# Probability-value products on all 128 columns of TensorE: shared values as fp32r halves for both heads, fox values side by side in F32

## The chip, the cores and the metric

The kernel runs on one core of a Trainium2 chip. Its time is the device time of one execution in microseconds (us), three runs before the change: 3118.08 us median (3116.48 to 3119.01). The profiled execution took 3118.62 us. Engines: PE is TensorE (matmul, with PEld for its weight loads), DVE VectorE, ACT ScalarE, POOL GpSimd, SP the engine that issues the DMAs.

## The reference

The reference is a whole model for 512 tokens of width 1024: a first block (state-space branch, spatial gating, cross attention, feed-forward) and a second block of two layers with four branches each. The change touches three of those four branches, which are attentions with 8 heads of 64 columns. All compute softmax(q k^T + bias) v:

```python
def forgetting_attention(q, k, v, f_logit, f_bias):     # v: one set of 64 columns per head
    ...
    p = jax.nn.softmax(jnp.where(causal[None, None], logits, neg), axis=-1)
    return jnp.einsum('bhqs,bshd->bqhd', p.astype(v.dtype), v)
def dsa_attention(q, k, v, qi, ki, wi):                  # v: one set for all 8 heads, causal, top 128 keys
    ...
    return jnp.einsum('bhqk,bqkd->bqhd', p.astype(vg.dtype), vg)
def sliding_window_gqa(q, k, v, sinks):                  # v: one set for 4 heads, window of 128 keys
    ...
    out = jnp.einsum('bngrqk,bnkgd->bnqgrd', (p / denom).astype(vband.dtype), vband)
```

"Shared values" are those of the second (called DSA here) and the third (sliding window): both heads of a pair multiply their own probabilities with the same 64 columns. The first ("fox") has values of its own for each head.

## The kernel before

Almost all large products are done with split operands. An F32 matrix is cut into a high part that fits TensorE's fp32r format and a low part with the rest (`split`, line 164: a copy on ACT writes the high part, a subtraction on DVE or POOL the low one), and `mm3` (lines 187 to 191) issues three fp32r products (high x high, high x low, low x high) in place of one in F32. `gemm_b` and `gemm_a` run this over the contraction; weights come by DMA as "raw" and are split on the fly.

Each of the two layers of the second block is `mix2` (line 1302). It projects the 512 tokens into queries, keys and values, and runs the four branches. Softmax work is written as Python generators (`attend`, line 952), one per pair of heads; `pump` takes a few steps of the waiting generators between two projections, and `drain` runs one to its end. The build then orders the instructions of each engine with a timeline model of its own, so that the program order mixes the steps of several generators with the projections. Each engine takes its instructions strictly in that order.

`attend` treats the 512 queries in four chunks c of 128. For a chunk it computes the scores of both heads into a PSUM bank "sc" each (`score`: lines 1081 and 1082 for fox, 1093 and 1094 for the others), masks and takes the maximum on DVE (line 968), exponentials and their sum on ACT (through line 124), normalises on DVE (line 982), transposes the probabilities in blocks of 128x128 on PE (line 995), copies them out of PSUM on ACT (line 998, tile probT), and multiplies by the values (line 1003). A causal chunk c has c+1 key blocks, a window chunk two (the first one). In line 1003 the stationary operand is a value block of one head (128 keys x 64 columns), the moving operand 128 transposed probabilities, both F32; head 0 writes partitions 0 to 63 and head 1 partitions 64 to 127 of one bank "pv", which is held for the four chunks of a pair and evicted once, with one `split` of 128x512 (lines 1008 and 1009).

The values: fox values come from `natural` into four tiles h; the shared ones lie in msc, which holds 204 columns per chunk (64 for DSA, two sets of 64 for the window, then 4 and 8 columns for other uses).

The buffers that matter: PSUM banks "mm" (4, results of projections), "sc" (3, scores and transposes) and "pv" (1); SBUF tiles of 128x512 "g" (52, long-lived), "tmp" (10) and probT (3). A projection for the rotary branches leaves its "mm" bank by four copies on ACT (`rope`, line 925) and one product on DVE (line 927).

Of the kernel before, what the change touches and what calls it, by code (L numbers as in the profile page):

```python
# [9 lines left out]
F32 = mybir.dt.float32  # L10
F32R = mybir.dt.float32r
AF = mybir.ActivationFunctionType
ALU = mybir.AluOpType
# [17 lines left out]
NSLOT = 52  # L31
# [40 lines left out]
class Builder:  # L72
# [879 lines left out]
    def attend(self, ys, pair, score, mask, init, value, blocks, sinks=None):  # L952

        nc = self.nc
        pv = None
        pend = None
        for c in list(range(CHUNKS)) + [None]:
# [28 lines left out]
            if pend is not None:  # L986
                pc, bl, pt = pend
                if pv is None:
                    pv = self.bank("pv")
                n = len(bl)  # L990
                tt = []
                for i in range(2):
                    tr = self.bank("sc")
                    for j in range(n):
                        nc.tensor.transpose(tr[:, j * P:(j + 1) * P], pt[i][:, j * P:(j + 1) * P],  # L995
                                            self.ident)
                    ptT = self.t(self.ap, [P, S], "probT", bufs=3)
                    nc.scalar.copy(ptT[:, :n * P], tr[:, :n * P])  # L998
                    tt.append(ptT)
                yield  # L1000
                for j, b in enumerate(bl):
                    for i in range(2):
                        nc.tensor.matmul(pv[i * 64:(i + 1) * 64, pc * P:(pc + 1) * P],  # L1003
                                         value(i, b), tt[i][:, j * P:(j + 1) * P],
                                         start=j == 0, stop=j == n - 1)
                yield
            pend = nxt
        yh, yl = self.g(F32R), self.g(F32R)
        self.split(yh, yl, pv)
        ys[pair] = (yh, yl)  # L1010
        yield

    def fox_bias(self, l, msc):
# [5 lines left out]
        self.add(f, msc[:, :, 196:204], self.vec(f"fb{l}")[:, None, :].to_broadcast(n4))  # L1019
# [35 lines left out]
    def fox_pair(self, ys, pair, pq, pk, va):  # L1055
# [23 lines left out]
        def score(i, c, ps, k0, nk):  # L1079
# [5 lines left out]
                           lambda i, b: va[b][:, pair * P + i * 64:pair * P + i * 64 + 64],  # L1085
                           lambda c: list(range(c + 1)))

    def rope_pair(self, ys, pair, q, hh, ll, mask, init, value, blocks, sinks=None):
# [7 lines left out]
        return self.attend(ys, pair, score, mask, init, value, blocks, sinks)  # L1096

    def select(self, si, hh, ll, msc):
# [3 lines left out]
        nc.vector.tensor_scalar(wi, msc[:, :, 192:196], 0.0625, None, ALU.mult)  # L1102
# [199 lines left out]
    def mix2(self, l):  # L1302
# [19 lines left out]
        msc = self.t(ap, [P, CHUNKS, 204], "msc")  # L1322
# [276 lines left out]
```

## Time and profile before

| what | value |
|---|---|
| time, median of three runs | 3118.08 us |
| profiled execution, its own time | 3118.62 us |
| its span, first to last instruction | 3116.7 us |
| PE busy | 3031.5 us (97%) |
| DVE busy | 1884.2 us (60%) |
| ACT busy | 1352.9 us (43%) |
| POOL busy | 974.6 us (31%) |
| DMA | 287.10 MB, 29.6% of 16 engines' span |

A matmul's record in the trace is longer than the distance to the next one, because matmuls are pipelined: what one costs PE is read from the starts of its neighbours. An F32 matmul leaves two records, one in fp32r leaves one. "Idle before" is the time in which an engine stood still ahead of a group, with what ended it.

### The profile page before, as it was taken

Reading aid. Unit: us, or ns where it says so; the run is one execution under the profiler, and the core shown is the slowest. Engines: PE = TensorE matmul, PEld = TensorE weight load, DVE = VectorE, ACT = ScalarE, POOL = GpSimd, SP = SyncE. Lnnn points to the kernel's source line nnn. Section 1 sums busy time; section 2 is a strip of 40 time slices with the busy share of each in tenths; the row PEclk is TensorE's granted clock in tenths of the full one; section 3 lists DMA queues with packets and bytes.
Section 4 is the critical chain, followed back from the end, with each engine's and each line's share of the span. In section 5 each row is a group of like instructions: output and inputs, shape, how many; then the busy total and the mean of one; then the engine's idle time right before and its main releaser. Section 6 shows DMA issues by size and latency. Waiting matters only on the chain.

```text
span 3116.7 us, 39233 instructions
## 1 busy us (share of the span) xinstructions
PE 3031.5 (97%) x14922; PEld 2481.6 (80%) x14922; DVE 1884.2 (60%) x3423; ACT 1352.9 (43%) x2278; POOL 974.6 (31%) x594
## 2 busy tenths in 40 slices
PE   8998999999999999999999999999999999999998
PEld 6877878888887777778888888888677778888887
DVE  7899454454455596455456665548845455465575
ACT  5523343332224475646334333356555452343343
POOL 3234243210014442345454000054333445610011
PEclk9999999999999999999999999999999999999999
DMA  5223343223333321222223323242211222333332
GB/s 161 75 80 95 102 146 105 95 88 102 101 90 94 102 75 55 68 78 82 78 88 122 95 91 105 81 133 78 68 55 61 92 75 78 122 96 100 95 96 80
DMA packets 98075, 287.10 MB, mean 92 GB/s; under 512 B 11984, under 2 KB 20432, under 8 KB 97888
## 3 DMA queue, kind: packets, MB, share of 16 engines
q1 hardware_dynamic: 97888, 284.61, 29.6%
q8 instruction: 117, 1.92, 0.3%
q14 instruction: 70, 0.57, 0.1%
HBM read 274.64 MB, written 9.93 MB: 91 GB/s over the span
## 4 chain that ended last, share of the span: by engine, by line
PE 82%; DVE 11%; ACT 2%; DMA 2%; issue 2%; POOL 1%; SPq 0%; DVEq 0%; ACTq 0%; POOLq 0%
PE psmm L189 24%; PE psmm L190 24%; PE psmm L191 24%; DVE tmp L112 3%; PE pspv L1003 2%; DVE g L112 2%; PE pssc L995 1%; DVE g L1128 1%; DVE m L1127 1%; PE pssc L1093 1%; DVE tmp L1217 1%; PE pssc L1094 1%; DVE s5t L112 0%; PE pspv L791 0%; PE pssc L759 0%
## 5 line engine op out<-in xcount | busy, mean ns | idle before, releaser
L191 PE MATMUL psmm<-g,lo 128*128 128x512 f32 (+1 forms) x3456 | 1346.8, 390 | 4.0 <-POOL lo L112 4.0
L190 PE MATMUL psmm<-g,hi 128*128 128x512 f32 (+1 forms) x3456 | 1348.2, 390 | 1.5 <-DVE g L171 1.5
L189 PE MATMUL psmm<-g,hi 128*128 128x512 f32 (+1 forms) x3456 | 1346.4, 392 | 2.3 <-ACT g L167 1.3
L167 ACT CAST hi<-raw 128x1024 fp32r<-128x1024 f32 (+3 forms) x506 | 507.6, 1005 | 1035.3 <-PE psmm L190 748.5
L112 POOL TENSOR_TENSOR lo<-raw,hi 128x1024 fp32r<-128x1024 f32 (+1 forms) x259 | 630.6, 2436 | 1008.8 <-ACT hi L167 849.2
L191 PEld LDWEIGHTS psmm<-g,lo 128*128 128x128 f32 x3456 | 650.3, 188 | 138.4 <-POOL lo L112 5.3
L189 PEld LDWEIGHTS psmm<-g,hi 128*128 128x128 f32 x3456 | 650.2, 188 | 135.4 <-ACT hi L167 3.1
L190 PEld LDWEIGHTS psmm<-g,hi 128*128 128x128 f32 x3456 | 650.8, 188 | 132.3 <-issue 2.6
L112 POOL TENSOR_TENSOR tmp<-tmp,tmp 128x512 f32<-128x512 f32 (+1 forms) x121 | 166.8, 1381 | 1019.1 <-DVE tmp L1419 570.7
L112 DVE TENSOR_TENSOR lo<-raw,hi 128x1024 fp32r<-128x1024 f32 (+2 forms) x247 | 298.0, 1207 | 90.7 <-ACT hi L167 90.6
L112 DVE TENSOR_TENSOR tmp<-psmm,g 128x512 f32<-128x512 f32 x236 | 161.4, 688 | 295.9 <-PE psmm L191 248.3
L189 PE MATMUL psmm<-hi,g 128*128 128x512 f32 (+1 forms) x384 | 144.5, 384 | 16.4 <-ACT g L124 11.1
L1445 DVE SCALAR_TENSOR_TENSOR g<-psmm,g 128x512 f32<-128x512 f32 x88 | 60.7, 690 | 151.7 <-PE psmm L191 151.7
L124 ACT ACTIVATE prob<-prob,nmx 128x128 f32<-128x128 f32 (+2 forms) x192 | 102.5, 535 | 106.7 <-DVE nmx L968 105.9
L190 PE MATMUL psmm<-lo,g 128*128 128x512 f32 (+1 forms) x384 | 146.5, 384 | 2.4 <-POOL lo L112 2.4
L191 PE MATMUL psmm<-hi,g 128*128 128x512 f32 (+1 forms) x384 | 145.2, 382 | 0.0
L112 DVE TENSOR_TENSOR g<-tmp,g 64x512 fp32r<-64x512 f32 (+1 forms) x162 | 130.5, 806 | 14.1 <-ACT g L167 11.0
L124 ACT ACTIVATE tmp<-tmp 128x512 f32<-128x512 f32 (+1 forms) x138 | 84.2, 613 | 111.4 <-DVE tmp L112 98.5
L1419 DVE SCALAR_TENSOR_TENSOR tmp<-tmp,vec,tmp 128x511 f32<-128x511 f32 (+1 forms) x176 | 131.0, 746 | 2.0 <-ACT tmp L124 0.6
L998 ACT COPY probT<-pssc 128x128 f32<-128x128 f32 (+2 forms) x192 | 69.8, 397 | 88.3 <-PE pssc L995 83.3
L189 PEld LDWEIGHTS psmm<-hi,g 128*128 128x128 f32 x384 | 75.1, 196 | 29.2 <-ACT g L124 11.1
L982 DVE TENSOR_SCALAR prob<-prob,sm 128x128 f32<-128x128 f32 (+2 forms) x192 | 93.2, 527 | 2.5
(276 smaller groups left out, 3117.6 us busy)
## 6 DMA issues: line engine op xcount, KB each, us to landing
raw<-w_up SPq DMA_DIRECT2D x110, 512.0 KB, 3.5
raw<-w_gates SPq DMA_DIRECT2D x64, 512.0 KB, 3.5
raw<-w_down SPq DMA_DIRECT2D x72, 384.0 KB, 3.1
raw<-w_rope SPq DMA_DIRECT2D x40, 512.0 KB, 3.6
raw<-w_branch SPq DMA_DIRECT2D x32, 512.0 KB, 3.5
raw<-w_out SPq DMA_DIRECT2D x24, 512.0 KB, 3.6
raw<-w_gate SPq DMA_DIRECT2D x22, 512.0 KB, 3.7
raw<-w_fox SPq DMA_DIRECT2D x16, 512.0 KB, 3.5
```

Of the source, the lines that this page charges most:

```text
L112: (eng or self.nc.vector).tensor_tensor(out, a, b, op)
L124: self.nc.scalar.activation(out, in_, func, **k)
L167: nc.scalar.copy(hi, src)
L189: mm(out, sh, mh, start=start, stop=False)
L190: mm(out, sh, ml, start=False, stop=False)
L191: mm(out, sl, mh, start=False, stop=stop)
L982: nc.vector.tensor_scalar(pt[i][:, :nk], pt[i][:, :nk], sm[:, i:i + 1], None, ALU.mult)
L995: nc.tensor.transpose(tr[:, j * P:(j + 1) * P], pt[i][:, j * P:(j + 1) * P], self.ident)
L998: nc.scalar.copy(ptT[:, :n * P], tr[:, :n * P])
L1003: nc.tensor.matmul(pv[i * 64:(i + 1) * 64, pc * P:(pc + 1) * P], value(i, b), tt[i][:, j * P:(j + 1) * P], start=j == 0, stop=j == n - 1)
L1419: nc.vector.scalar_tensor_tensor(o[:, sh:], u[:, :S - sh], w, o[:, sh:], ALU.mult, ALU.add)
L1445: self.nc.vector.scalar_tensor_tensor(self.x[d], ps, 0.5, self.x[d], ALU.mult, ALU.add)
```

## The change

Shared values are split once, when they are projected, into high and low parts that lie side by side: 128 stationary columns in fp32r (tile vhl). The probabilities of both heads are transposed into one bank, next to each other (256 moving columns per key block), and split as well: a high part probT by a copy on ACT, a low part by a subtraction on DVE. One product with the high and one with the low probabilities then give, for both heads at once, high values in partitions 0 to 63 and low values in 64 to 127 of the "pv" bank; the two halves are added on the way out. Fox values stay F32, but the two heads' value columns stand side by side as 128 stationary columns, each head's 128 probabilities are multiplied with both, and of the result the half that belongs to the head is taken. As outputs take twice the room, the "pv" bank holds two chunks and is evicted twice per pair. There are five probT tiles, and four "g" tiles fewer.

```diff
-NSLOT = 52
+NSLOT = 48
+NPT = 5
...
-    def attend(self, ys, pair, score, mask, init, value, blocks, sinks=None):
+    def attend(self, ys, pair, score, mask, init, value, blocks, shared, sinks=None):
...
+        dt = F32R if shared else F32
...
             if pend is not None:
                 pc, bl, pt = pend
-                if pv is None:
+                n = len(bl)
+
+                tt = []
+                for j0 in range(0, n, 2):
+                    tr = self.bank("sc")
+                    w = min(2, n - j0) * 2 * P
+                    for k in range(w // P):
+                        j, i = j0 + k // 2, k % 2
+                        nc.tensor.transpose(tr[:, k * P:(k + 1) * P], pt[i][:, j * P:(j + 1) * P],
+                                            self.ident)
+                    th = self.t(self.ap, [P, S], "probT", dt, bufs=NPT)
+                    tl = self.t(self.ap, [P, S], "probT", dt, bufs=NPT) if shared else None
+                    nc.scalar.copy(th[:, :w], tr[:, :w])
+                    if shared:
+                        self.sub(tl[:, :w], tr[:, :w], th[:, :w].bitcast(F32))
+                    tt.append((th, tl))
+                yield
+                u = pc % 2
+                if u == 0:
                     pv = self.bank("pv")
-                n = len(bl)
-                tt = []
-                for i in range(2):
-                    tr = self.bank("sc")
-                    for j in range(n):
-                        nc.tensor.transpose(tr[:, j * P:(j + 1) * P], pt[i][:, j * P:(j + 1) * P],
-                                            self.ident)
-                    ptT = self.t(self.ap, [P, S], "probT", bufs=3)
-                    nc.scalar.copy(ptT[:, :n * P], tr[:, :n * P])
-                    tt.append(ptT)
+                if shared:
+                    out = pv[:, u * 256:(u + 1) * 256]
+                    for j, b in enumerate(bl):
+                        for z in range(2):
+                            nc.tensor.matmul(out, value(b), tt[j // 2][z][:, j % 2 * 256:j % 2 * 256 + 256],
+                                             start=j == z == 0, stop=j == n - 1 and z == 1)
+                else:
+                    for i in range(2):
+                        out = pv[:, u * 256 + i * P:u * 256 + i * P + P]
+                        for j, b in enumerate(bl):
+                            a = j % 2 * 256 + i * P
+                            nc.tensor.matmul(out, value(b), tt[j // 2][0][:, a:a + P],
+                                             start=j == 0, stop=j == n - 1)
                 yield
-                for j, b in enumerate(bl):
-                    for i in range(2):
-                        nc.tensor.matmul(pv[i * 64:(i + 1) * 64, pc * P:(pc + 1) * P],
-                                         value(i, b), tt[i][:, j * P:(j + 1) * P],
-                                         start=j == 0, stop=j == n - 1)
-                yield
+                if u:
+                    if yh is None:
+                        yh, yl = self.g(F32R), self.g(F32R)
+                    cs = slice(pc * P - P, pc * P + P)
+                    v = "p (u i n) -> p u i n"
+                    p4 = pv.rearrange(v, u=2, i=2)
+                    two = lambda x: x.rearrange("p (u n) -> p u n", u=2)
+                    if shared:
+                        t, y = self.tmp()[0:64], self.tmp()[:, :256]
+                        nc.scalar.copy(t, pv[64:128])
+                        t4 = t.rearrange(v, u=2, i=2)
+                        for i in range(2):
+                            self.add(two(y[i * 64:i * 64 + 64]), p4[0:64, :, i], t4[:, :, i])
+                        self.split(yh[:, cs], yl[:, cs], y)
+                    else:
+                        for i in range(2):
+                            r = slice(i * 64, i * 64 + 64)
+                            self.split(two(yh[r, cs]), two(yl[r, cs]), p4[r, :, i])
+                    yield
             pend = nxt
-        yh, yl = self.g(F32R), self.g(F32R)
-        self.split(yh, yl, pv)
         ys[pair] = (yh, yl)
-        yield
...
-                           lambda i, b: va[b][:, pair * P + i * 64:pair * P + i * 64 + 64],
-                           lambda c: list(range(c + 1)))
+                           lambda b: va[b][:, pair * P:(pair + 1) * P],
+                           lambda c: list(range(c + 1)), False)
...
-        msc = self.t(ap, [P, CHUNKS, 204], "msc")
-        self.natural(I["w_misc"][l], x, [msc[:, c] for c in range(CHUNKS)], 204, 2)
+        msc = self.t(ap, [P, CHUNKS, 12], "msc")
+        vhl = self.t(ap, [P, CHUNKS, 3, 2, 64], "vhl", F32R)
+        banks = self.gemm_a(I["w_misc"][l], x, 204, 2)
+        self.pump(self.rate)
+        for c in range(CHUNKS):
+            self.split(vhl[:, c, :, 0], vhl[:, c, :, 1], banks[c][:, :192].rearrange("p (v d) -> p v d", v=3),
+                       scale=self.rc[:, c:c + 1])
+            self.act(msc[:, c], banks[c][:, 192:204], AF.Copy, scale=self.rc[:, c:c + 1])
+        vals = lambda b, n: vhl[:, b, n].rearrange("p z d -> p (z d)")
```

The new order of the program on PE is shown at three places of the first layer. Lines 190 to 192 of the changed kernel are the old 189 to 191, 1003 is now the transposes' line (old 995), 1131 and 1132 are the old scores 1093 and 1094; 1019 and 1026 are the new products.

First, on PE, the first product of the first DSA pair; before:

```order
L190 MATMUL psmm_9829<-g_9753,hi_9825 128x512
L191 MATMUL psmm_9829<-g_9752,lo_9826 128x512
L1003 MATMUL pspv_9843<-probT_9846,msc_7999 64x128
L1003 MATMUL pspv_9843<-probT_9850,msc_7999 64x128
L190 MATMUL psmm_9935<-g_9753,hi_9825 128x512
```

and with the change:

```order
L191 MATMUL psmm_9842<-g_9702,hi_9838 128x512
L192 MATMUL psmm_9842<-g_9701,lo_9839 128x512
L1019 MATMUL pspv_9863<-probT_9859,vhl_8000 128x256
L1019 MATMUL pspv_9863<-probT_9860,vhl_8000 128x256
L191 MATMUL psmm_9950<-g_9702,hi_9838 128x512
```

One product per head with 64 columns became one per part of the probabilities, with 128 columns and both heads in the 256 moving columns.

Second, on PE, the second chunk of the second fox pair, where the head's products stood apart and a score product lay between; before:

```order
L1003 MATMUL pspv_8945<-probT_9055,h_8124 64x128
L1081 MATMUL pssc_9070<-g_8617,g_8615 128x512
L1082 MATMUL pssc_9070<-g_8621,g_8619 128x512
L191 MATMUL psmm_9871<-g_7705,lo_9875 128x512
L1003 MATMUL pspv_8945<-probT_9060,h_8124 64x128
L1003 MATMUL pspv_8945<-probT_9055,h_8125 64x128
L1003 MATMUL pspv_8945<-probT_9060,h_8125 64x128
```

and with the change:

```order
L192 MATMUL psmm_9769<-g_7711,hi_9772 128x512
L1026 MATMUL pspv_8960<-probT_9064,h_8133 128x128
L1026 MATMUL pspv_8960<-probT_9064,h_8134 128x128
L1026 MATMUL pspv_8960<-probT_9064,h_8133 128x128
L1026 MATMUL pspv_8960<-probT_9064,h_8134 128x128
L190 MATMUL psmm_9769<-g_7721,hi_9772 128x512
```

The number of products is the same, each writes 128 partitions, and they now follow each other.

Third, on PE, the third DSA pair between its second and its last chunk of scores (g_9315 and g_9316 before, g_9309 and g_9310 after, are its queries); before:

```order
L1093 MATMUL pssc_10337<-g_7895,g_9316 128x384
L1094 MATMUL pssc_10337<-g_7897,g_9316 128x384
L995 MATMUL pssc_10346<-idn_71,prob_10281 128x128
L1003 MATMUL pspv_10298<-probT_10301,msc_7999 64x128
L1003 MATMUL pspv_10298<-probT_10305,msc_7999 64x128
L995 MATMUL pssc_10346<-idn_71,prob_10281 128x128
L995 MATMUL pssc_10351<-idn_71,prob_10282 128x128 x2
L190 MATMUL psmm_10813<-g_7706,hi_10816 128x512
L191 MATMUL psmm_10813<-g_7705,lo_10817 128x512
L189 MATMUL psmm_10813<-g_7711,hi_10816 128x512
```

and with the change:

```order
L1131 MATMUL pssc_10383<-g_7895,g_9309 128x384
L1132 MATMUL pssc_10383<-g_7897,g_9309 128x384
L1131 MATMUL pssc_10387<-g_7895,g_9310 128x384
L1132 MATMUL pssc_10387<-g_7897,g_9310 128x384
L1003 MATMUL pssc_10369<-idn_71,prob_10316 128x128
L1019 MATMUL pspv_10376<-probT_10372,vhl_8000 128x256
L1003 MATMUL pssc_10410<-idn_71,prob_10332 128x128
L1131 MATMUL pssc_10436<-g_7895,g_9309 128x512
L1132 MATMUL pssc_10436<-g_7897,g_9309 128x512
L1003 MATMUL pssc_10410<-idn_71,prob_10333 128x128
L1003 MATMUL pssc_10410<-idn_71,prob_10332 128x128
L1003 MATMUL pssc_10410<-idn_71,prob_10333 128x128
```

Where 24 projection products followed the transposes, the next chunk's scores and transposes now follow at once, and from the second head's first score of the pair to its last chunk's transposes no projection product stands on PE.

## Rows read from the trace of the kernel before

**Rows 1.** The page: busy tenths of PE in 40 slices of the span, its granted clock in tenths of full speed, and the chain that ended last by engine and by line.

```profile
PE   8998999999999999999999999999999999999998
...
PEclk9999999999999999999999999999999999999999
...
PE 82%; DVE 11%; ACT 2%; DMA 2%; issue 2%; POOL 1%; SPq 0%; DVEq 0%; ACTq 0%; POOLq 0%
PE psmm L189 24%; PE psmm L190 24%; PE psmm L191 24%; DVE tmp L112 3%; PE pspv L1003 2%; DVE g L112 2%; PE pssc L995 1%; DVE g L1128 1%; DVE m L1127 1%; PE pssc L1093 1%; DVE tmp L1217 1%; PE pssc L1094 1%; DVE s5t L112 0%; PE pspv L791 0%; PE pssc L759 0%
```

**Rows 2.** Busy time in stretches with fox (1100 and 2155) and with shared values (1222): length, then busy us and instructions of PE, PEld, DVE, ACT and POOL, granted clock, DMA share, GB/s; then PE's waits in 1100 to 1225 and 2150 to 2280: us in total, times, longest.

```profile
1100.00:1222.00 122.00, 116.58 (x629) 89.58 (x627) 103.26 (x279) 78.26 (x167) 42.49 (x22) 1.00 0.21 65
1222.00:1585.00 363.00, 362.81 (x1941) 289.88 (x1941) 188.05 (x463) 174.95 (x368) 164.65 (x94) 1.00 0.24 76
2155.00:2277.00 122.00, 112.99 (x611) 86.24 (x610) 102.30 (x270) 75.65 (x161) 41.01 (x20) 1.00 0.20 63
...
PE pssc L995 <- DVE prob L982: 1.2, 1, 1.2
...
PE pssc L995 <- DVE prob L982: 4.8, 4, 2.2
```

**Rows 3.** Groups of PE's instructions by line and form: out<-in, rows*columns of the weights, moving operand, count, busy us, mean ns, idle before.

```profile
L1003 PE MATMUL pspv<-probT,msc 128*64 128x128 f32 x544 | 55.8, 287 | 0.0
L1003 PE MATMUL pspv<-probT,h 128*64 128x128 f32 x320 | 33.3, 286 | 4.6 <-ACT probT L998 4.1
```

**Rows 4.** PE's timeline around two stretches of old products, of four and of sixteen records: start in us, length, what.

```profile
1227.13 0.40 PE L191 MATMUL psmm<-g,lo 128*128 128x512 f32 x1
1227.46 0.44 PE L1003 MATMUL pspv<-probT,msc 128*64 128x128 f32 x4
1227.83 0.50 PE L190 MATMUL psmm<-g,hi 128*128 128x512 f32 x1
1228.16 0.39 PE L191 MATMUL psmm<-g,lo 128*128 128x512 f32 x1
1228.39 0.40 PE L190 MATMUL psmm<-g,hi 128*128 128x512 f32 x1
...
1248.32 0.39 PE L191 MATMUL psmm<-g,lo 128*128 128x512 f32 x1
1248.64 1.09 PE L1003 MATMUL pspv<-probT,msc 128*64 128x128 f32 x16
1249.66 0.33 PE L1093 MATMUL pssc<-g,g 128*128 128x128 f32 x1
1249.83 0.28 PE L1094 MATMUL pssc<-g,g 128*128 128x128 f32 x1
1249.94 0.33 PE L1093 MATMUL pssc<-g,g 128*128 128x256 f32 x1
```

**Rows 5.** PE's timeline where full-width products of the new forms stand already: fp32r with 256 moving columns (344), and F32 with 128 moving columns (line 1167, in the retention branch).

```profile
344.42 0.28 PE L189 MATMUL psmm<-g,hi 128*128 128x256 f32 x1
344.53 0.28 PE L190 MATMUL psmm<-g,hi 128*128 128x256 f32 x1
344.65 0.28 PE L191 MATMUL psmm<-g,lo 128*128 128x256 f32 x1
...
1536.76 0.39 PE L190 MATMUL psmm<-g,hi 128*128 128x512 f32 x1
1536.98 0.38 PE L1167 MATMUL pspv<-tmp,tmp 128*128 128x128 f32 x2
1537.20 0.56 PE L1171 MATMUL pspv<-h,tmp 128*128 128x64 f32 x4
1537.60 0.44 PE L1167 MATMUL pspv<-tmp,tmp 128*128 128x128 f32 x2
1537.87 0.56 PE L1171 MATMUL pspv<-h,tmp 128*128 128x64 f32 x4
```

**Rows 6.** Groups of DVE and ACT by line and form: out<-in, count, busy us, mean ns, idle before. Lines 968 and 982 are masking with maxima and normalising, "g<-pspv" the old eviction, 998 the copy of transposed probabilities, 925 a rotary copy.

```profile
L968 DVE CUSTOM_DVE_ANT_0 prob<-pssc,cst 128x128 f32<-128x128 f32 x32 | 9.1, 288 | 46.7 <-PE pssc L1094 36.4 <-PE pssc L1082 10.3
L968 DVE CUSTOM_DVE_ANT_0 prob<-pssc,g 128x256 f32<-128x256 f32 x16 | 6.5, 422 | 7.0 <-PE pssc L1094 7.0
L968 DVE CUSTOM_DVE_ANT_0 prob<-pssc,g 128x384 f32<-128x384 f32 x16 | 8.7, 554 | 2.5 <-PE pssc L1094 2.3
L968 DVE CUSTOM_DVE_ANT_0 prob<-pssc,g 128x512 f32<-128x512 f32 x16 | 10.7, 686 | 6.9 <-PE pssc L1094 6.9
L982 DVE TENSOR_SCALAR prob<-prob,sm 128x128 f32<-128x128 f32 x48 | 14.2, 333 | 0.6
L982 DVE TENSOR_SCALAR prob<-prob,sm 128x256 f32<-128x256 f32 x80 | 43.2, 582 | 1.0
L982 DVE TENSOR_SCALAR prob<-prob,sm 128x384 f32<-128x384 f32 x32 | 19.4, 646 | 0.3
L982 DVE TENSOR_SCALAR prob<-prob,sm 128x512 f32<-128x512 f32 x32 | 16.6, 559 | 0.5
L112 DVE TENSOR_TENSOR g<-pspv,g 128x512 fp32r<-128x512 f32 x32 | 22.0, 686 | 47.5 <-ACT g L167 47.5
L998 ACT COPY probT<-pssc 128x512 f32<-128x512 f32 x32 | 17.7, 586 | 25.4 <-PE pssc L995 21.9 <-PE pspv L1003 3.5
L925 ACT COPY tmp<-psmm 32x512 f32<-32x512 f32 x160 | 92.4, 578 | 2.4
```

More of the change, by code (lines that the diff above doesn't have):

```diff
@@ L949, in stack_k @@
         return hh, ll
-    def attend(self, ys, pair, score, mask, init, value, blocks, sinks=None):
+    def attend(self, ys, pair, score, mask, init, value, blocks, shared, sinks=None):
         nc = self.nc
+        dt = F32R if shared else F32
         pv = None
         pend = None
+        yh = yl = None
         for c in list(range(CHUNKS)) + [None]:
@@ L1006, in attend @@
-                yield
+                    th = self.t(self.ap, [P, S], "probT", dt, bufs=NPT)
[4 more added lines that the diff above has]
+                    tt.append((th, tl))
+                yield
+                u = pc % 2
+                if u == 0:
+                    pv = self.bank("pv")
@@ L1018, in fox_bias @@
         a = self.t(ap, n4, "fa")
-        self.add(f, msc[:, :, 196:204], self.vec(f"fb{l}")[:, None, :].to_broadcast(n4))
+        self.add(f, msc[:, :, 4:12], self.vec(f"fb{l}")[:, None, :].to_broadcast(n4))
         self.nc.vector.scalar_tensor_tensor(a, f, -1.0, f, ALU.mult, ALU.min)
@@ L1094, in score @@
             nc.tensor.matmul(ps, q[i][:, qs], ll[:, k0:k0 + nk], start=False, stop=True)
-        return self.attend(ys, pair, score, mask, init, value, blocks, sinks)
+        return self.attend(ys, pair, score, mask, init, value, blocks, True, sinks)
     def select(self, si, hh, ll, msc):
@@ L1101, in select @@
         wi = self.t(ap, [P, CHUNKS, 4], "wi")
-        nc.vector.tensor_scalar(wi, msc[:, :, 192:196], 0.0625, None, ALU.mult)
+        nc.vector.tensor_scalar(wi, msc[:, :, 0:4], 0.0625, None, ALU.mult)
         self.masks = {}
@@ L1347, in mix2 @@
                                      lambda c: self.maskc(c) if c == 0 else self.masks[c],
-                                     lambda i: 3e38, lambda i, b: msc[:, b, 0:64],
+                                     lambda i: 3e38, lambda b: vals(b, 0),
                                      lambda c: list(range(c + 1))))
@@ L1364, in mix2 @@
                 lambda i, j=j: nsk[:, 2 * j + i:2 * j + i + 1],
-                lambda i, b, hg=hg: msc[:, b, 64 + hg * 64:128 + hg * 64],
+                lambda b, hg=hg: vals(b, 1 + hg),
                 lambda c: [c] if c == 0 else [c - 1, c],
```

1 line of the change is left out of this document (removed).

## The prediction

> **What bounds the kernel now.** I read the page first [rows 1]: the slices show TensorE (PE) at 9 tenths or more almost everywhere and its granted clock at full speed, and the chain that ended last is 82% PE, three quarters of it the split-precision products of lines 189 to 191. What PE is given less to do is therefore worth its time, in a stage where PE does not wait. Next I cut out the stretches of the two attention layers in which probability times value (line 1003) runs [rows 2]. From 1222 to 1585 us PE is busy for 362.8 of 363 us, and the answer on its waits there is empty; VectorE (DVE) is at 188 of 363, with room. From 1100 to 1222, and in the second layer from 2155 to 2277, DVE is busy for 103 and 102 of 122 us, and PE waits for it (1.2 and 4.8 us on the normalised probabilities alone). So the first kind of stretch pays a saving on PE out in full as long as the order keeps PE fed, the second does not.
>
> **What the old products cost.** Their group [rows 3] lists 544 records with shared values and 320 with the forgetting-attention ("fox") values at 286 to 287 ns each, but a pipelined record's length is not its price, so I took starts in the timeline [rows 4]. Around four records: from the start of the product before (1227.13) to that of the second product after (1228.16) is 1.03 us; two plain 512-column products at 0.23 (1228.16 to 1228.39) belong to others, which leaves 0.57. Around sixteen records, 1248.32 to 1249.83 is 1.51; less 0.23 and one 128-column score product (0.11, to 1249.94) leaves 1.17. The records stand in the two 64-column halves of the array for the two heads and go side by side: sixteen make eight steps, four make two. So a step costs (1.17 - 0.57) / 6 = 0.10 us, and entering and leaving a stretch of such records 0.57 - 0.20 = 0.37.
>
> The program order of before has 139 such stretches with 518 steps (a product without a partner counts two): 92 with 328 for shared values, 47 with 190 for fox. That is 92 x 0.37 + 328 x 0.10 = 66.8 us for shared and 36.4 us for fox, together 103.2 us, half of it entering and leaving.
>
> The Trainium skill, "TensorEngine Tiling (Array Packing)", Key Properties, says that a change of tiling mode, not of tile alone, drains the engine; the 0.37 us of [rows 4] agrees with that. The Trainium skill, "TensorE: Matmul & The Clock Gate", Part 3, says that products of at most 64 columns put into different column groups run concurrently, which speaks against this change: by that rule alone the halves already fill the array, as the eight steps of [rows 4] bear out. What it would make of the time is the last rival.
>
> **What the new products cost.** Shared: 272 products with 128 stationary columns, 256 moving columns, both in fp32r. The same form stands elsewhere at 0.115 to 0.12 us start to start, straight behind others [rows 5] (from 344.42 on), so 272 x 0.12 = 32.6 us. Fox: 160 products with 128 stationary and 128 moving columns in F32, two records each. The same form at line 1167 [rows 5] takes 0.22 us for two records (1536.98 to 1537.20) and starts 0.22 us behind the plain product before it, so there is no entry cost: 160 x 0.22 = 35.2 us. Its second pair of records took 0.27 (1537.60 to 1537.87), which would make 43 us; I take 0.22, since fox products follow each other. PE is spared 103.2 - 67.8 = 35 us (27 to 36), nearly all of it with shared values, in the stretch where PE never waits. Fox alone is about even. Scores and transposes keep number and form.
>
> **What is added, and what hides it.** DVE and ACT get the low parts of the transposed probabilities (80 subtractions, 0.42 to 0.69 us each by columns [rows 6]), two evictions of the output bank per pair in place of one, and the split of shared values. By layer that is 28 x 0.69 + 12 x 0.42 = 24 us of low parts, 48 x 0.42 = 20 of additions and subtractions in evictions, less 8 x 0.69 of the old ones, plus 6 for (b): 45 us of DVE; in the 1222 stretch 175 us of DVE stand idle per layer, so as a sum it is covered. What is not covered is where the new order lets it stand in a row:
>
> (a) Third pair of DSA heads. In the new order the scores of this pair's chunks, from the second head's first one on, its transposes and products stand behind each other on PE with no projection product between, while before up to 24 stood between two chunks. The projections cannot fill in: four of them have their result in the four "mm" banks, and the order empties these only behind the attention work on DVE (the rotary tiles now share the ten "tmp" buffers with the evictions). DVE must do in that time, by [rows 6], 2 x (0.29 + 0.42 + 0.55 + 0.69) = 3.9 us of masking and maxima, 2 x (0.33 + 0.58 + 0.65 + 0.56) = 4.2 of normalising, 0.42 + 2 x 0.69 = 1.8 of low parts and, at 256 columns, four additions and one subtraction of evictions, 5 x 0.42 = 2.1: 12 us. PE has there 20 transposes and 10 products at 0.11 to 0.12 and 12 scores between 0.11 and 0.23 by their columns [rows 4], some 5.5. Then a bank must be emptied, four ACT copies of 0.58 = 2.3. PE waits 12 - 5.5 + 2.3 = 8.8 us a layer, 18 in both. Bounds: 0, if DVE gets ahead, and 22, if every hop between ACT and DVE shows.
>
> (b) Fox. Per pair the bank is now emptied in two times two subtractions of 64x256 in place of one of 128x512 (0.69). No row shows 64x256; by columns it lies between the 0.29 (128) and the 0.69 (512) of line 968, and the nearest is 0.42: 4 x 0.42 - 0.69 = 1.0 us more a pair, 4 a layer. In the first half of the pairs DVE sets the pace [rows 2], so 2 a layer, 4 in all (0 to 8). The value split adds 4 subtractions a layer in the same stretch, covered in part: 1 (0 to 4).
>
> (c) A second product of a block waits for copy and subtraction (0.59 + 0.69 us) where one copy did before. In most places the order has transposes or projections between the two: 1 us (0 to 6).
>
> The pool of 48 instead of 52 "g" buffers moves instructions in the first block too, by a few products around its S5 output; I put it at nothing (2 us either way).
>
> Sum against the profiled execution (3118.62, its span of 3116.7 and 1.9 around it that nothing here touches; the median is 3118.08, 0.5 lower): -35 + 18 + 5 + 1 = -11, so 3107.6, and 3107 as a median.
>
> **Rivals.**
> 1. The saving arrives almost whole: DVE runs ahead at (a) and PE waits no more than 6 us in all. For it: DVE's 175 idle us a layer. Against it: the order at (a). 3118 - 35 + 6 = 3089.
> 2. No change: the waits at (a) and (b) reach their upper ends (22 + 8 + 4 + 6 = 40), or 30 of it: 3113 to 3123. For it: DVE is already the pace of fox.
> 3. Slower through the one "pv" bank. It is now handed on 47 times (23 before), each time only after a copy from PSUM and two additions (0.59 + 2 x 0.42 = 1.4 us); a product that asks for it too early stops all behind it on PE. It decides from a mean wait of 35 / 47 = 0.75 us on; at 1.2 us it costs 56, so 3118 - 35 + 56 = 3139. Against it: in the new order only four hand-overs have under 1.5 us of PE work between, by these durations.
> 4. Slower because the 0.37 us belong to any stretch of such products (a wait on the probabilities, say) and not to the half array. The new order has 125 shared and 34 fox stretches: 159 x 0.37 = 59 us on top of 67.8, against 103.2, so +24 and 3142. Against it: the full-width F32 products of [rows 5] enter at no cost. (By the Trainium skill's rule on column groups, cited above, the old halves would be the better form; this is the rival that it stands for.)
>
> **How the numbers follow.** Forecast 0.55, rival 1 0.20, rival 2 0.15, rivals 3 and 4 0.06 and 0.04. A change under 0.2% (6 us) can't be told from none. Faster: forecast and rival 1 less the forecast's own upper edge, 0.73; same 0.17; slower 0.10. The forecast's own range is 3098 to 3113; to hold 8 in 10 it must reach into rivals 1 and 2: 3088 to 3119.
>
> **What would show it.** Right: shared products 0.12 us apart with no 0.2 us gaps at their edges; fox records 0.11 apart; PE waiting on DVE or ACT for some 9 us in the third DSA pair of both layers, with the rope copies behind; total PE wait up by about 24 us. Wrong: gaps of 0.3 us at the new products (rival 4), waits of line 1019 or 1026 on the eviction all along the pairs (rival 3), or no wait at the third pair (rival 1).

## The result, and the profile after

The changed kernel takes 3134.32 us, median of four runs (3132.92 to 3135.77). The kernel before, in runs beside them on the same chip, took 3118.55 (3116.48 to 3120.06). The ratio is 1.0051, with a 95% interval of 1.0034 to 1.0068: half a per cent slower, where 3107 (3088 to 3119) was forecast. The profiled execution took 3132.92 us, with a span of 3131.1.

From the page of the changed kernel: busy time of the engines, and, answering to [rows 1], the chain that ended last by engine and by line.

```profile
PE 3019.7 (96%) x14650; PEld 2515.7 (80%) x14650; DVE 1977.0 (63%) x3615; ACT 1378.8 (44%) x2294; POOL 978.4 (31%) x594
...
PE 80%; DVE 12%; ACT 3%; issue 2%; DMA 1%; POOL 1%; SPq 0%; DVEq 0%; POOLq 0%; ACTq 0%
PE psmm L190 24%; PE psmm L191 24%; PE psmm L192 24%; DVE tmp L113 3%; DVE g L113 2%; DVE g L1166 1%; PE pssc L1003 1%; DVE m L1165 1%; DVE prob L989 1%; PE pspv L1019 1%; PE pspv L1026 1%; DVE tmp L1255 1%; DVE prob L975 1%; DVE s5t L113 0%; PE pssc L1193 0%
```

PE is busy for 3019.7 us (3031.5 before), so the work on PE fell by 11.8 only; span less busy time, which is PE's idle time, rose from 85.2 to 111.4. That is the whole result: -11.8 + 26.2 = +14.4 us of span. To place it, both traces are cut at events that exist in both: first transpose of a fox probability, last fox product, end of the layer's branches. First the kernel before (length, then busy us and instructions of PE, PEld, DVE, ACT, POOL, granted clock, DMA share, GB/s), fox and the rest of layer 0, then of layer 1:

```profile
1107.50:1224.20 116.70, 111.17 (x615) 85.06 (x614) 96.99 (x265) 72.74 (x158) 38.28 (x19) 1.00 0.20 64
1224.20:1693.00 468.80, 467.69 (x2401) 376.19 (x2398) 241.79 (x525) 216.24 (x430) 223.34 (x123) 1.00 0.27 85
2157.80:2278.50 120.70, 111.69 (x616) 85.37 (x614) 100.38 (x266) 74.01 (x160) 39.63 (x20) 1.00 0.20 62
2278.50:2700.00 421.50, 420.28 (x2187) 336.68 (x2184) 217.00 (x502) 197.34 (x405) 201.69 (x113) 1.00 0.26 80
```

and the same four stretches with the change:

```profile
1109.20:1234.90 125.70, 115.42 (x618) 96.48 (x617) 110.25 (x291) 80.11 (x170) 39.43 (x21) 0.97 0.19 59
1234.90:1704.40 469.50, 458.92 (x2262) 381.78 (x2261) 275.46 (x598) 223.86 (x427) 225.22 (x123) 0.99 0.27 85
2168.40:2294.40 126.00, 114.56 (x618) 95.22 (x617) 110.50 (x292) 80.10 (x170) 39.67 (x21) 0.99 0.19 59
2294.40:2714.20 419.80, 408.23 (x2047) 340.47 (x2047) 250.98 (x576) 205.36 (x402) 203.60 (x113) 1.00 0.26 80
```

The fox stretches grew by 9.0 and 5.3 us: that is nearly the whole loss (the rows' starts show another 1.7 us ahead of the first fox stretch). Of these 14.3 us, 7.2 are idle time of PE and 7.1 busy time. The stretches with shared values, where the gain was to be, came out about even (+0.7 and -1.7): PE's busy time there fell by 8.8 and 12.1 and its idle time rose by 9.5 and 10.4. The granted clock, 1.00 in all four before, fell to 0.97 and 0.99 in three. An estimate from the fox stretches' clocks, 0.03 x 125.7 + 0.01 x 126.0 = 5 us, puts most of the added busy time there down to the clock.

PE's longest waits in the changed kernel (us in total, times, longest):

```profile
PE pssc L1003 <- DVE prob L989: 16.7, 15, 2.3
...
PE psmm L190 <- ACT g L168: 10.7, 10, 2.1
PE pssc L1119 <- DVE nmx L975: 7.9, 7, 2.3
...
PE pspv L1019 <- ACT probT L1007: 3.2, 4, 1.1
```

Transposes wait for normalised probabilities 16.7 us in all (6.0 before), and fox's scores 7.9 us for DVE's maxima (1.1 before). Products of line 190 wait 10.7 us for a high part that ACT writes (line 168). Of these, 9.4 us lie in the two attention layers, and 7.3 are four waits in the stretches with shared values, in which a branch waits for the last evicted output of its pairs.

### The profile page after: what moved, and what is told of

It reads as the page before. It is cut to its first block, busy times and chain, and to the rows that moved or that the text cites. A ratio compares the mean times of both kernels' runs of the same rounds, so it can differ in the third digit from the quotient of the medians.

```text
span 3131.1 us, 38799 instructions
## 1 busy us (share of the span) xinstructions
PE 3019.7 (96%) x14650; PEld 2515.7 (80%) x14650; DVE 1977.0 (63%) x3615; ACT 1378.8 (44%) x2294; POOL 978.4 (31%) x594
## 4 chain that ended last, share of the span: by engine, by line
PE 80%; DVE 12%; ACT 3%; issue 2%; DMA 1%; POOL 1%; SPq 0%; DVEq 0%; POOLq 0%; ACTq 0%
PE psmm L190 24%; PE psmm L191 24%; PE psmm L192 24%; DVE tmp L113 3%; DVE g L113 2%; DVE g L1166 1%; PE pssc L1003 1%; DVE m L1165 1%; DVE prob L989 1%; PE pspv L1019 1%; PE pspv L1026 1%; DVE tmp L1255 1%; DVE prob L975 1%; DVE s5t L113 0%; PE pssc L1193 0%
## 5 line engine op out<-in xcount | busy, mean ns | idle before, releaser
L190 PE MATMUL psmm<-g,hi 128*128 128x512 f32 (+1 forms) x3456 | 1349.0, 392 | 19.4 <-ACT g L168 10.7
L190 PEld LDWEIGHTS psmm<-g,hi 128*128 128x128 f32 x3456 | 652.8, 189 | 153.2 <-ACT g L168 13.5
L113 DVE TENSOR_TENSOR g<-tmp,g 64x512 fp32r<-64x512 f32 (+2 forms) x194 | 160.5, 827 | 16.2 <-ACT g L168 13.4
L926 ACT COPY tmp<-psmm 32x512 f32<-32x512 f32 x160 | 92.6, 579 | 2.4
```

Source lines behind the costliest of these rows:

```text
L113: (eng or self.nc.vector).tensor_tensor(out, a, b, op)
L190: mm(out, sh, mh, start=start, stop=False)
L926: nc.scalar.copy(xs[k * 32:k * 32 + 32], bk[(k ^ 1) * 32:(k ^ 1) * 32 + 32])
```

## The experiments

Each run was timed in three rounds beside the kernel before (3115.8 to 3118.5 us by group of runs); a ratio is to that. Times of different groups are best compared by their ratios.

### Each half of the change alone, and the pool alone

e1 calls the old generator for fox and keeps the rest of the change; e2 keeps the old generator for shared values; e3 is one number; e4 moves one line.

```diff
e1  fox_pair:   return self.attend_old(...)        # shared values: the new attend
e2  fox_pair:   return self.attend_new(..., False) # shared values: the old attend, NSLOT = 52, 3 probT
e3  -NSLOT = 52
    +NSLOT = 48
e4  branch:  -for d in range(lead):
             +for d in range(lead - 1):
                  gate(d)
              self.drain(*gens)
             +gate(lead - 1)
```

> Only the shared values go the new way; fox keeps the old products and its one eviction per pair. Theory A (the change spares PE about 20 us, nearly all with shared values, and adds 31 us of waits: 8 in fox, 11 where the first branch product waits for a pair's last eviction, 12 in the third DSA pair): fox's waits go, 3126 us (3122 to 3129). Theory B (the loss is all in the shared part: evictions through copy and additions): 3133 or more. Theory C (fox is the whole loss and shared values alone bring the forecast saving): under 3112.

Measured: 3130.6 us, 1.0031 (1.0020 to 1.0041).

> Only fox goes the new way; the shared values keep the old products, 52 g buffers and three probT. Theory A: PE is about even there and DVE's extra evictions show as waits: 3124 us (3120 to 3128). Theory B: 3118, as before. Theory C: 3130 or more.

Measured: 3135.6 us, 1.0056 (1.0041 to 1.0071).

> The kernel before with 48 g buffers in place of 52 and nothing else. Forecast of the prediction and theories A to C: 3118 us, 2 either way. Theory D (the smaller pool is what costs: it moves the order and binds transfers to evictions): 3124 us or more.

Measured: 3127.9 us, 1.0036 (1.0022 to 1.0050).

> The changed kernel, but a branch finishes its attention pairs ahead of its last leading gate product in place of behind it, so that 24 projection products stand between the last evictions and the branch product that waits for them. Theory A: of the 10.7 us in ten waits of the branch product on the high part of the evicted output 8 or more go: 3125 us (3122 to 3128). Theory B (the waits only move to the gate's place, since DVE's work per pair is what is late): 3132 to 3136.

Measured: 3131.1 us, 1.0042 (1.0027 to 1.0057).

All four went against theory A, which I held then. 48 buffers, with nothing else changed, cost 9.3 us, more than half of the whole loss (theory D). Shared values alone, with these 48 buffers, cost 12.1, between theories A and B. Fox alone, with 52, costs 17.1, more than fox does within the change; its stretches took 129.8 and 128.2 us. The parts don't add up, so something in fox must depend on how the work happens to fall in time. In e4 the waits on high parts fell from 9.4 to 2.1 us in the attention layers, but those on normalised probabilities rose from 16.7 to 22.0: the wait mostly moved.

The fox stretch of layer 0 in e3, to be held against the first row of the kernel before above:

```profile
1107.90:1231.20 123.30, 114.24 (x616) 87.48 (x614) 101.91 (x266) 75.01 (x160) 39.37 (x20) 0.97 0.20 60
```

266 instructions of DVE (265 before) took 101.9 us in place of 97.0. The groups of DVE show which: in the kernel before, in that stretch (count, busy us, mean ns, idle before),

```profile
L112 DVE TENSOR_TENSOR g<-tmp,g 64x512 fp32r<-64x512 f32 x15 | 12.3, 823 | 0.4
L1127 DVE MAX8 m<-g 128x8 f32<-128x512 f32 x14 | 9.6, 684 | 0.1
L112 DVE TENSOR_TENSOR h<-psmm,g 128x512 f32<-128x512 f32 x8 | 5.4, 680 | 1.8 <-PE psmm L191 1.8
L982 DVE TENSOR_SCALAR prob<-prob,sm 128x512 f32<-128x512 f32 x8 | 4.6, 614 | 0.1
```

in e3,

```profile
L112 DVE TENSOR_TENSOR g<-tmp,g 64x512 fp32r<-64x512 f32 x15 | 14.6, 972 | 0.4
L982 DVE TENSOR_SCALAR prob<-prob,sm 128x512 f32<-128x512 f32 x8 | 6.5, 853 | 0.1
L112 DVE TENSOR_TENSOR h<-psmm,g 128x512 f32<-128x512 f32 x8 | 5.4, 678 | 2.0 <-PE psmm L191 2.0
```

and in e2, the worst:

```profile
L113 DVE TENSOR_TENSOR g<-tmp,g 64x512 fp32r<-64x512 f32 x16 | 20.1, 1255 | 0.4
L1226 DVE MAX8 m<-g 128x8 f32<-128x512 f32 x14 | 9.6, 684 | 0.1
L1050 DVE TENSOR_SCALAR prob<-prob,sm 128x512 f32<-128x512 f32 x8 | 6.7, 874 | 0.1
L113 DVE TENSOR_TENSOR g<-pspv,g 64x256 fp32r<-64x256 f32 x14 | 5.9, 418 | 1.6 <-ACT g L168 1.4
L113 DVE TENSOR_TENSOR h<-psmm,g 128x512 f32<-128x512 f32 x8 | 5.5, 683 | 1.4 <-PE psmm L192 1.3
```

Instructions that read PSUM keep their length (680, 678, 683 ns), and so does MAX8, which reads one operand from SBUF (684 and 684). The subtractions with two operands in SBUF stretch, the same form from a mean of 823 to 1255 ns, and so do the normalisations, which scale from SBUF to SBUF (614 to 853 and 874). The changed kernel's timeline shows what they meet; this is the third DSA pair, where PE waits 1.95 us for a transpose's operand:

```profile
1285.25 2.36 POOL L113 TENSOR_TENSOR lo<-raw,hi 128x1024 fp32r<-128x1024 f32 x1 [5.01 <-ACT hi L168]
...
1286.17 1.71 DVE L989 TENSOR_SCALAR prob<-prob,sm 128x128 f32<-128x128 f32 x2
...
1287.74 0.33 PE L1003 MATMUL pssc<-idn,prob 128*128 128x128 f32 x1 [1.95 <-DVE prob L989]
```

POOL splits a weight's low part from 1285.25 to 1287.61. DVE's two normalisations of 128 columns, 0.33 us each by [rows 6], take 1.71, and end 0.27 us behind POOL. The Trainium skill, "SBUF — State Buffer", Who interferes with whom, says that DVE and GpSimd share one pair of SBUF ports, that an instruction of DVE with two SBUF inputs contends there with one of GpSimd that reads SBUF, as does one in certain modes, which a scaling can use, and that the one that comes second is blocked, not slowed. An instruction of DVE with at most one SBUF input, outside these modes, does not contend by the same section of the Trainium skill. The lengths above agree: what stretches has two SBUF inputs or is a scaling, and what reads PSUM, or one operand as MAX8 does, keeps its length.

### The price of the product forms, and shorter instructions on POOL

```diff
e5  -nc.tensor.matmul(out, value(b), tt[j // 2][z][:, j % 2 * 256:j % 2 * 256 + 256], ...)
    +for i in range(2): for each block: for z in range(2):
    +    nc.tensor.matmul(pv[z*64:z*64+64, <128 columns of head i>],
    +                     value(b)[:, z*64:z*64+64].bitcast(F32), tt[j // 2][z][:, a:a + P].bitcast(F32), ...)
e6, e7 (weights, in the kernel after and before)
    -self.split(hi, lo, raw, eng=gpsimd)
    +nc.scalar.copy(hi, raw)
    +for a in range(0, width, 256):  self.sub(lo[:, a:a+256], raw[:, a:a+256], hi[:, a:a+256], gpsimd)
e8  e1 and the edit of e4, NSLOT = 50, NPT = 3
```

> The changed kernel, with the products of shared values back in the old form (64 stationary columns, 128 moving, F32, the two halves of the array side by side, two steps a block) and everything else as changed: same tiles, low parts, evictions. It leaves out the cross products of high and low parts and the precision that they bring. Theory R (the prediction's ruler holds: 0.37 us per stretch and 0.10 per step): 125 stretches and 272 steps are 73 us against 32.6, so 3165 to 3178 us. Theory S (a stretch costs about 0.25 us, as starts alone suggest): 58 against 32.6, 3152 to 3163. Theory N (waits cover the form): under 3145.

Measured: 3198.1 us, 1.0261 (1.0245 to 1.0276), 63.8 above the changed kernel. The expectation has a slip: a block is four F32 products of two records each, so 544 steps and not 272. With them the ruler gives 122 x 0.37 + 544 x 0.10 = 99.5 us, 67 more than 32.6. So the new form is worth having; how much in place of the kernel before's, which had 328 steps, is shown by e9 and e14 below.

> The changed kernel, with the low parts of weights, 128x1024 subtractions of 2.4 us on POOL, issued as four of 128x256. Theory P (DVE sets the pace in the fox stretch, and its subtractions and normalisations from SBUF to SBUF wait for a whole POOL subtraction when they meet one): the pieces cut such a wait from up to 1.4 us to under 0.6, the fox stretches shrink by 3 to 6 us each: 3121 to 3129. Theory Q (the collisions are not what makes it late, or pieces cost POOL more than they give): 3132 to 3142.

Measured: 3091.7 us, 0.9911 (0.9895 to 0.9928).

> The kernel before with the same four pieces on POOL. Theory P: DVE is the pace there too, 3110 to 3116. Theory Q: 3117 to 3126.

Measured: 3081.3 us, 0.9883 (0.9868 to 0.9898).

Theory P by far more than it claimed: 42.6 and 36.5 us, since the pieces help in the whole kernel and not only in fox. DVE's busy time over the whole execution fell from 1977.0 to 1864.2 us in the changed kernel (3615 instructions in both) and from 1884.2 to 1782.0 in the kernel before (3423 in both). The change stays behind, by 10.4 us. The fox stretch of layer 0 in e6:

```profile
1096.10:1212.20 116.10, 111.36 (x618) 94.19 (x617) 100.79 (x282) 80.72 (x171) 47.77 (x60) 1.00 0.21 64
```

The one of layer 1 takes 116.2 us there; in e7 the two take 114.4 and 113.7, so with POOL in pieces the change costs fox 4.2 us where it cost 14.3, and at the full clock. The build orders the program anew for the pieces; how much of these gains is order was not separated.

> Shared values the new way, fox as before, 50 g buffers and three probT, and each branch finishes its attention pairs ahead of its last leading gate product. Theory A (per layer 17 us spared with shared values, 9 given back in the third DSA pair, nothing at the branch products, fox as in the kernel before): 3102 to 3110. Theory D (any move of the order costs fox what the 48 buffers cost it): 3111 to 3120. Worse than 3122 speaks against both.

Measured: 3135.1 us, 1.0056 (1.0041 to 1.0071). Worse than both theories allow. Its fox stretches are shorter than e1's (119.9 and 123.6 us against 124.6 and 123.5); the loss lies behind them (936.1 and 844.9 us to the next fox stretch and to the end, against 931.3 and 836.2). Why e4's edit costs that in this order stays open.

### The parts again, with POOL in pieces

e9 is e3, e10 is e1, e11 is e2, each with the pieces of e6; e12 is e7 with pieces of 128.

> The kernel before with 48 g buffers and POOL's low parts in four pieces. Theory P (the smaller pool cost 9 us only because the order it gives lets DVE's subtractions meet POOL's long ones): within 3 us of the kernel before with pieces, 3078 to 3085 us. Theory D (the pool itself makes work wait): 3088 or more.

Measured: 3089.4 us, 0.9916 (0.9902 to 0.9931).

> Shared values the new way, fox as before, 48 g buffers, POOL in four pieces. Theory A (34 us spared on PE by shared values, 16 given back in the third DSA pair with its lower clock and 9 at the branch products that wait for a pair's last eviction): 3070 to 3077 us, under the kernel before with pieces. Theory E (the waits of the shared part eat all of its saving): 3080 to 3087.

Measured: 3089.5 us, 0.9915 (0.9899 to 0.9932).

> Fox alone the new way, 52 g buffers, POOL in four pieces. Theory P (of the 17 us that fox alone cost, DVE's collisions with POOL are the larger part): 3084 to 3090 us. Theory F (two evictions per pair through one output bank cost it by themselves): 3094 or more.

Measured: 3085.7 us, 0.9905 (0.9890 to 0.9920).

> The kernel before with POOL's low parts in eight pieces of 128x128. Theory P: what is left of the collisions halves again, 3072 to 3079 us. Theory Q: eight starts on POOL cost what they give, 3080 to 3090.

Measured: 3077.8 us, 0.9878 (0.9863 to 0.9893).

Against e7's 3081.3, fox's new form now costs 4.4 us where it cost 17.1 without pieces. By the ratios, since e7 was timed in another group, it is 0.0022, or 7 us; its fox stretches (117.5 and 116.9 us) are 6.3 longer than e7's. So collisions were the larger part, and what is left is near the prediction's 5. The pool still costs 8.1 (by the ratios 10), against theory P, and the shared values add nothing to that (e10 is e9 within 0.1, above what either of its theories allowed). Pieces of 128 and of 256 can't be told apart (0.9878 and 0.9883).

The pool's cost can be placed. Fox in layer 0 in e9, and ten us of it:

```profile
1092.00:1210.40 118.40, 113.25 (x616) 87.56 (x614) 96.51 (x264) 74.60 (x160) 47.87 (x61) 0.97 0.20 63
...
1189.00:1199.00 10.00, 9.43 (x54) 7.80 (x52) 4.53 (x19) 5.07 (x16) 0.00 (x0) 0.66 0.01 2
```

the same in e7:

```profile
1088.10:1202.50 114.40, 109.95 (x615) 85.16 (x614) 95.47 (x264) 74.39 (x160) 49.77 (x61) 1.00 0.21 65
...
1185.00:1195.00 10.00, 9.70 (x67) 7.24 (x64) 5.95 (x23) 5.87 (x19) 0.00 (x0) 1.00 0.01 2
```

Work and DVE's time agree; 4.0 us more, of which 10 x (1 - 0.66) = 3.4 are PE at the lower of its two clock levels for a while. The order that 48 buffers give has PE's waits elsewhere, one of 1.3 and one of 0.6 us just ahead of the fall and in it. (Another 3.9 us are lost before fox begins, as the rows' starts show, and 3.6 in fox of layer 1, where the clock was 0.99, so that the clock is there at most a third of it. These parts add up to the 11.4 us between the two profiled executions, not to the 8.1 between the medians; the cause of the 3.9 stays open.) The changed kernel has the same in more places; ten-us pieces of its trace, each 1.00 in the same ten us of the kernel before except for the first, which had 0.83:

```profile
1020.00:1030.00 10.00, 8.56 (x57) 8.56 (x58) 9.83 (x17) 6.07 (x10) 0.00 (x0) 0.70 0.40 146
1130.00:1140.00 10.00, 8.38 (x35) 7.00 (x36) 9.93 (x21) 9.77 (x17) 5.61 (x6) 0.83 0.13 48
...
1290.00:1300.00 10.00, 8.25 (x37) 6.13 (x37) 7.36 (x21) 7.31 (x17) 0.73 (x1) 0.72 0.05 18
2350.00:2360.00 10.00, 7.81 (x40) 6.37 (x41) 7.81 (x22) 7.72 (x18) 1.29 (x1) 0.83 0.01 2
```

0.17 of ten us are up to 1.7 us of PE at full speed. Each of these pieces follows on, or holds, a wait of 1.9 us or more. That the wait lowers the clock is not shown by this: the kernel before has a wait of 2.2 us in fox of layer 1, and e7 one of 1.9 in fox of layer 0, both with 1.00 behind them.

### The ring of temporary tiles

The prediction's step (a) laid the third DSA pair's waits on the rotary tiles that share the "tmp" ring with the evictions. e13 gives the evictions tiles of their own, in the changed kernel; e14 does it in e10, e15 is e14 with 49 buffers and pieces of 128, e16 is e13 with pieces of 128.

```diff
-t, y = self.tmp()[0:64], self.tmp()[:, :256]
+t, y = self.t(self.ap, [64, S], "evt", bufs=1), self.t(self.ap, [P, 256], "evy", bufs=1)
-NPT = 5
+NPT = 3
```

> The changed kernel, with the two tiles of the shared eviction in buffers of their own in place of the "tmp" ring that the rotary tiles use, and three probT in place of five to make room. In its order projection products stand between the chunks of the third DSA pair again. Theory A (the third pair's waits and the lower clock behind them, 16 us in both layers, come from that shared ring): 3118 us (3113 to 3123). Theory E (DVE and ACT have the same work for fewer us of PE, so the waits only move to the other pairs): 3128 to 3136.

Measured: 3137.8 us, 1.0067 (1.0051 to 1.0084).

> Shared values the new way with their eviction tiles in buffers of their own, fox as before, 48 g buffers, three probT, POOL in four pieces of 256. Theory A: 3073 us (3068 to 3078), 16 under the same kernel with the shared ring. Theory E: 3084 to 3092.

Measured: 3075.0 us, 0.9869 (0.9855 to 0.9884).

> As the kernel before this one, with 49 g buffers and POOL in pieces of 128. Theory A: 3068 us (3061 to 3074), under the kernel before with such pieces (3077.8). Theory E: 3078 or more.

Measured: 3060.9 us, 0.9824 (0.9810 to 0.9839).

> The changed kernel whole (fox too), eviction tiles in buffers of their own, three probT, POOL in pieces of 128. Theory A: 3072 us (3067 to 3078). Theory E: 3083 or more.

Measured: 3064.3 us, 0.9833 (0.9818 to 0.9848).

In e13 the third pair's waits are gone: from 1245 to 1340 us PE waits for nothing, where the changed kernel waited 5.2 us over the same work. That bears out the link, though e13 has three probT too. But the time did not follow, and the fox stretch grew (129.4 us, not followed up). In the window pairs a new wait of 4.3 us stands:

```profile
1374.78 2.38 POOL L113 TENSOR_TENSOR lo<-raw,hi 128x1024 fp32r<-128x1024 f32 x1
1374.99 2.19 DVE L113 TENSOR_TENSOR es<-vec,nmx 128x2 f32<-128x2 f32 x1
...
1378.42 2.34 POOL L113 TENSOR_TENSOR lo<-raw,hi 128x1024 fp32r<-128x1024 f32 x1
...
1378.64 2.54 DVE L989 TENSOR_SCALAR prob<-prob,sm 128x256 f32<-128x256 f32 x2
...
1380.97 1.17 PE L1003 MATMUL pssc<-idn,prob 128*128 128x128 f32 x4 [4.29 <-DVE prob L989]
```

A DVE addition of two columns takes 2.19 us, until POOL is through; the normalisation behind it meets POOL again. With POOL in pieces the ring's share comes free: e14 is 14.4 us under e10 (which differs by its five probT too). The stretch behind fox in layer 0, in e9 with the old products and in e14 with the new ones, both at full clock:

```profile
1210.40:1677.70 467.30, 467.03 (x2400) 376.33 (x2396) 209.67 (x524) 216.02 (x430) 256.31 (x321) 1.00 0.27 85
```

```profile
1213.40:1671.70 458.30, 455.00 (x2264) 380.73 (x2260) 240.68 (x604) 225.39 (x430) 256.73 (x321) 1.00 0.27 87
```

PE's work fell by 12.0 us, 3.0 of it given back as idle time. In layer 1 it is 467.0 against 455.3, so 24 us in both layers: the cleanest measure of what the new products are worth.

The best version is e15, 3060.9 us: shared values the new way, fox as before, tiles of their own, short pieces on POOL. It beats the kernel before by 1.8% and e12, the kernel before with such pieces, by 16.9 us (0.9824 against 0.9878). The whole change with the same two mends, e16, is 13.5 us under e12. Both came out at or under the low end of their theory's range, and the shares of the 49 buffers, the three probT and the pieces of 128 were not separated.

## Why the prediction was wrong, point by point

By stretches, the prediction's terms come to about -15 us with shared values (-34 of products, +18, +1) and +4 in fox (-1 and +5). Measured are -1.0 and +14.3. So two steps failed: "PE is spared 35 us", which was sized too high and had no term for a lower clock, and (b), fox.

- **The new products' price** nearly held, and the fox products' did. Four shared ones between other work, and the group of the fox products:

```profile
1345.64 0.40 PE L192 MATMUL psmm<-g,lo 128*128 128x512 f32 x1
1345.87 0.64 PE L1019 MATMUL pspv<-probT,vhl 128*128 128x256 f32 x4
1346.35 0.22 PE L1131 MATMUL pssc<-g,g 128*128 128x128 f32 x1
```

```profile
L1019 PE MATMUL pspv<-probT,vhl 128*128 128x256 f32 x272 | 56.4, 297 | 4.1 <-ACT probT L1007 3.2 <-DVE probT L113 0.7 <-DVE tmp L113 0.2
L1026 PE MATMUL pspv<-probT,h 128*128 128x128 f32 x320 | 42.2, 278 | 0.4 <-DVE g L113 0.4
```

  0.48 us for four, 0.12 each, with no gap at the edges, and fox's waits of 0.4 us in all; the records of fox products start 0.11 apart. The waits on the eviction are 0.2 and 0.4 us: rivals 3 and 4 are out.
- **The old products' price, "0.37 us" for each of 92 stretches,** was too high for the kernel before: with 24 us spared and 32.6 for the new ones, the old cost 57 and not 66.8. I had read the ruler at two stretches [rows 4] and laid it on all. e5 agrees with it, though (64 measured, 67 by the ruler). The sum of 57 takes the new ones at their forecast price. An estimate that reads every stretch of the traces in the same way (from the start of the product before to that of the second one after, less what these two take elsewhere) gives about 63 us for the old ones and 37 for the new in e14, 26 apart: each price was some 4 us off, in the direction that made the forecast low. A single new product between two of 512 columns takes 0.13 us (median of 37 in the changed kernel). The 34 us of the forecast and the 24 measured with shared values make 10 of the 27 us by which the forecast was low.
- **(a) The third DSA pair** was right in place, and its waits were about half of the 8.8 us a layer that were forecast: 4.2 us (1284 to 1300) and 5.3 (2343 to 2360). With a lower clock beside them, worth up to 3.4 and 1.7 by the granted clocks, it comes near the forecast, but the clock was no term of it. e13 and e14 bear out the link to the ring. That POOL stretched one of its waits was not seen.
- **(b) Fox** failed as a step: "4 (0 to 8) + 1", counted from instructions at the lengths of [rows 6]. Measured +14.3. The extra instructions do cost about 5 (4.2 between e7 and e6, 4.4 to 7 between e7 and e11), and the 64x256 subtractions take the 0.42 us that were put down for them (0.418). The rest is that DVE's lengths are not its own. In fox DVE sets the pace, and its subtractions and scalings in SBUF wait for POOL; PE pays for that with waits and with its clock (idle time +7.2, of which 5 were forecast; busy time +7.1), and with POOL in pieces both are gone but for the 4.2; [rows 6] already had the sign of it, 128x512 normalised in 559 ns and 128x256 in 582.
- **"The pool of 48 ... at nothing (2 us either way)"** failed: 9.3 us alone (e3), 8.1 with pieces (e9). Its share in fox's 14.3 can't be told from the rest: e1 and e2 don't add up.
- **A wait not forecast:** the branch products behind a pair's last eviction, now a copy, two additions, a copy. The last window wait in layer 0:

```profile
1347.64 0.58 ACT L1038 COPY tmp<-pspv 64x512 f32<-64x512 f32 x1
...
1348.25 0.85 DVE L113 TENSOR_TENSOR tmp<-pspv,tmp 64x256 f32<-64x256 f32 x2
...
1349.21 0.39 ACT L168 CAST g<-tmp 128x256 fp32r<-128x256 f32 x1
...
1349.65 1.21 PE L190 MATMUL psmm<-g,hi 128*128 128x512 f32 x3 [2.10 <-ACT g L168]
```

  From the first copy to PE's start are 2.0 us in which nothing else is in order on PE. (c) had priced such a hop for the probabilities (forecast 1; 3.9 us of waits on probT at line 1019, 3.2 of them in the third DSA pair) but not for the output. Two such waits a layer are worth 7.3 us in all.
- **The sum.** PE's idle time was to rise by about 24 us and rose by 26.2. That this fits is in part luck: (a) cost 9.5 us of waits where 18 stood, and 7.3 came at the branch products, which had no term. The miss is in PE's busy time: it fell by 20.9 us in the stretches with shared values and rose by 7.1 in fox and 2.0 elsewhere, which leaves 11.8 where 35 stood. Rival 3's 3139 is near the result, but its place, waits on the output bank, holds 0.6 us. None of the rivals had a wait that depends on POOL, or the clock.

## What to carry to other kernels

Before you take an instruction's mean length from a group, look at its spread and at where its operands lie: on DVE, the lengths of subtractions with two operands in SBUF and of scalings within SBUF depended here on what POOL did meanwhile, and cutting long POOL instructions in pieces was worth 1.2% for one loop, more than the change itself. A saving on the busiest engine is worth what remains after the chain of the next engine is followed through it: look for rings of buffers that tie the two together, and for the last hop of each hand-over. When a kernel's order comes from a planner, run a neutral edit first (here four buffers fewer): it moved the time by 9.3 us, nearly as much as the forecast effect of 11.

## What the hardware showed that I had not expected

- A DVE addition of 128x2 took 2.19 us, and two 128x128 normalisations 1.71, beside a POOL subtraction of 2.4 us; a masking that reads PSUM kept 0.42 beside it, and PSUM readers of 512 columns a mean of 0.68 in the same stretches. Pieces of 256 columns on POOL took the kernel before from 3117.8 to 3081.3 us, though POOL's own busy time rises (from 38.3 to 49.8 us in a fox stretch); DVE's busy time fell from 1884.2 to 1782.0 us with as many instructions.
- In a kernel with PE busy for 96%, some waits of about 2 us were followed by PE at its lower clock level for a while, worth 1.7 to 3.0 us by the granted clock of ten us (0.83 to 0.70); others were not, as the kernel before's wait of 2.2 us in fox of layer 1 shows.
